# A decoder layer on one core: T4 is formed from T2 and B21, and the norms take their constant from a padded column

## The chip, the cores and the metric

The kernel runs on one core of one Trainium2 chip. Its time is the time on the device, in microseconds (us), from one launch to its end; the metric is the median over runs. Five engines work side by side, each through its own instructions in order: PE (TensorE, matmuls), DVE (VectorE, elementwise work), ACT (ScalarE, functions, copies and roundings), POOL (GpSimd) and SP (SyncE). SP, POOL and ACT also issue transfers (DMAs). An instruction that waits for another engine holds up everything behind it on its own engine.

## The reference

The depth is one, so of the four token mixers only the first (multi-scale causal pooling) runs, and then the gated ConvFFN. There are 1024 positions of 1024 features, a hidden width of 2816, and everything is float32.

```python
def rms_norm(x, g):
    xf = x.astype(jnp.float32)
    y = xf * lax.rsqrt(jnp.mean(xf * xf, axis=-1, keepdims=True) + EPS)
    return (y * g.astype(jnp.float32)).astype(x.dtype)

def pool_mixer(x, w, b, scale):
    ...
    for gi, w_len in enumerate(POOL_WINDOWS):          # 2, 4, 8, 16; 256 features each
        ...
        groups.append(window_sum / count - xf[..., gi * POOL_GROUP:(gi + 1) * POOL_GROUP])
    d = jnp.stack(groups, axis=2)
    y = jnp.einsum('bsgc,gcd->bsgd', d, w.astype(jnp.float32)).reshape(bsz, seq, D_MODEL) + b
    return (scale * y).astype(x.dtype)

def conv_ffn(x, w_in, conv_w, conv_b, w_out):
    h = causal_depthwise_conv(x @ w_in, conv_w, conv_b)
    val, gate = jnp.split(h, 2, axis=-1)
    return (jax.nn.silu(gate) * val) @ w_out

# the one layer
h = rms_norm(x, norm_mix_g)
x = x + pool_mixer(h, ...)
x = x + conv_ffn(rms_norm(x, norm_ffn_g), ...)
```

## The kernel before

**The first stage** takes the positions in eight tiles of 128, j = 0 to 7, in a software pipeline (the loop at L496): while tile j is normed and windowed, tile j-2 goes through the mixer's weights and tile j-4 becomes an operand of the feed-forward part. Per tile: ACT squares and sums x (`junk_a`, statistic `st_a`), DVE scales the window matrix by the norm (`bandr`), PE forms the window sums (`psd`), ACT copies them out (`dh`), PE multiplies by the pooling weights and adds the bias (`psy`), DVE adds x to give x1, which SP stores to DRAM (L268). x1 gets its own statistic (`junk_b`, `st_b`), DVE forms the normed tile (`n2`, printed as n_0 to n_7 in the program's order), and PE transposes it (`pst`). The last 16 rows of each tile reach the next one through a small extra product (`edge_band`, `ps_edges`, with a norm of its own, `st_e`).

**A norm's statistic** (`rstd_of`) is, with m the sum of squares: s = sqrt(m + D·EPS) on ACT (L158), m + D·EPS on DVE (L159), q = s·s + that on DVE (L161), 1/q on DVE (L162); s and 1/q are then used together as scales. There are eight of these for x (`a0` to `a7`), eight for x1 (`b0` to `b7`) and one for the edges (`e`).

**The second stage** multiplies by `w_in` with a seven-product scheme of the Strassen-Winograd kind. The normed, transposed activations are four quarters: B11 and B12 are the first 512 features for positions 0 to 511 and 512 to 1023, B21 and B22 the other 512 features. They lie in one tile, `n2f`. The operands are B11, B21, B22 and the sums T1 = B11 - B12, T3 = B22 - B12, T2 (minus the sum of B22 and T1, made in place of B22) and T4 = B22 - B21 + T1. In tiles j = 4 to 7, `ffn_operand` forms T1 from the first 512 features (L306), rounds it with ACT (L313) and leaves the remainder with DVE (L314): every operand is a rounded part and a remainder. It also forms T3 (L308) and B22 - B21 (L309), in 128-column pieces. T2 and T4 are made later, after the loop (L542 and L549), in two halves each.

The weights' side is 22 chunks n of 128 by 1024 (`win`), of which sums S1 to S4 are needed besides A11, A12 and A22. For the first two chunks these sums are made by accumulating DMAs that POOL issues (L336), later by DVE (L328). Each chunk's seven products (`step`, L374) go to the banks X, Y and Z; the first two chunks' products are interleaved so that P1 and P2 (B11, B21) come before the ones that need T1 (`Z<-T,S1s`), and T2, T3 and T4 last (L436 to L438). The chunk's outputs are then put together by DVE, convolved, gated and stored. **The third stage** does the same scheme with `w_out` (L731).

**What sets the order.** The code is written against a layer that records all operations and orders them itself, by a model of durations, holding to what the code asks with `issue_after`. A part that is left out or moved to another engine therefore changes the order of its neighbours too. Waits between engines come from that layer as well. The lines of the loop's end that the later steps turn on are:

```python
    for ks in halves:
        nc.vector.scalar_tensor_tensor(b22[:, ks], b22[:, ks], -1.0, t1[:, ks], op0=ALU.mult, op1=ALU.subtract)
        split_n(nops["T2"], b22[:, ks], ks=ks)
    event(7)
    event(8)
    for ks in halves:
        split_n(nops["T3"], t3[:, ks], ks=ks)
    for ks in halves:
        add(t4[:, ks], t4[:, ks], t1[:, ks])
        split_n(nops["T4"], t4[:, ks], ks=ks)
```

Of the kernel before, what the change touches and what calls it, by code (L numbers as in the profile page):

```python
# [7 lines left out]
F32 = mybir.dt.float32  # L8
F32R = mybir.dt.float32r
BF16 = mybir.dt.bfloat16  # L10
AF = mybir.ActivationFunctionType
ALU = mybir.AluOpType
PSUM = bass.MemoryType.PSUM

P = 128
S = 1024
D = 1024
# [8 lines left out]
EPS = 1e-6  # L26
# [15 lines left out]
XBUFS = 5  # L42
# [6 lines left out]
def trunk_kernel(ctx: ExitStack, tc: tile.TileContext, x, consts, par, rows, pool_w, w_in, w_out, out):  # L49
    nc = tc.nc  # L50
# [6 lines left out]
    hls = ctx.enter_context(tc.tile_pool(name="hls", bufs=1))  # L57
# [4 lines left out]
    pp = pre.enter_context(tc.tile_pool(name="pre", bufs=1))  # L62
# [17 lines left out]
        return t  # L80


    xs = {}

    def load_x(j):
        if j < 2 or j >= 2 + XBUFS:
            xs[j] = hls.tile([P, D], F32, tag="hl", name=f"x{j}", bufs=7)
        else:
            xs[j] = pp.tile([P, D], F32, tag="x", name=f"x{j}", bufs=XBUFS)
        nc.sync.dma_start(xs[j], x[j * P : (j + 1) * P, :])  # L90

    cst = pp.tile([P, BD], F32, tag="cst", name="cst")
# [7 lines left out]
    scale = rows_raw[:, 0, :GRP]  # L100
# [49 lines left out]
    ident = cst[:, ID:]  # L150

    marks = {}

    def rstd_of(src, name):
        junk = pp.tile([P, D], BF16, tag="junk", name=f"junk_{name}")
        st = pp.tile([P, 4], F32, tag="st", name=f"st_{name}", bufs=8)
        nc.scalar.activation(junk, src, AF.Square, accum_out=st[:, 0:1])
        marks[name] = nc.scalar.activation(st[:, 1:2], st[:, 0:1], AF.Sqrt, bias=eps_t).ins  # L158
        nc.vector.tensor_scalar(st[:, 0:1], st[:, 0:1], D * EPS, None, op0=ALU.add)  # L159

        nc.vector.scalar_tensor_tensor(st[:, 3:4], st[:, 1:2], st[:, 1:2], st[:, 0:1], op0=ALU.mult, op1=ALU.add)  # L161
        nc.vector.reciprocal(st[:, 2:3], st[:, 3:4])  # L162
        return st[:, 1:2], st[:, 2:3]
# [4 lines left out]
    bands, stats = {}, {}  # L168
# [84 lines left out]
    n2s = {}  # L253
# [16 lines left out]
            mixer_out_stats(j)  # L270

    def mixer_out_stats(j):
        n2s[j] = (n2s[j], rstd_of(n2s[j], f"b{j}"))

    def ffn_norm(j):
        x1, r = n2s[j]
# [13 lines left out]
    def ffn_operand(j):  # L290
        n2 = n2s.pop(j)
        ps = bank2(f"pst{j}")
        for c in range(NK):
            nc.tensor.transpose(ps[:, c * P : (c + 1) * P], n2[:, c * P : (c + 1) * P], ident)  # L294
        cols = slice(j * P, (j + 1) * P)
        ps3 = ps.rearrange("p (c s) -> p c s", c=NK)
        lo, hi = slice(0, 4), slice(4, 8)
        if j < NS // 2:
            split_n(nops["B11"], ps3[:, lo, :], cols)
            split_n(nops["B21"], ps3[:, hi, :], cols)  # L300
            nc.scalar.activation(n2f[:, :, cols], ps3, AF.Copy)
            return
        cols0 = slice(cols.start - NH, cols.stop - NH)
        b11, b12, b21, b22 = n2f[:, lo, cols0], ps3[:, lo, :], n2f[:, hi, cols0], n2f[:, hi, cols]
        nc.scalar.activation(b22, ps3[:, hi, :], AF.Copy)
        sub(b11, b11, b12)  # L306
        split_n(nops["T1"], b11, cols0)
        sub(n2f[:, lo, cols], b22, b12)  # L308
        sub(b21, b22, b21)  # L309

    def split_n(t, src, cols=slice(None), ks=slice(None)):
        h = t[:, 0, ks, cols]
# [11 lines left out]
    def sub(out, a, b):  # L324
        nc.vector.tensor_tensor(out, a, b, ALU.subtract)  # L325

    def add(out, a, b):
        nc.vector.tensor_tensor(out, a, b, ALU.add)  # L328
# [125 lines left out]

    def stat(j):
        if j in xs and j not in stats:
            stats[j] = rstd_of(xs[j], f"a{j}")

    scale_b = scale_rows()
    stat(0)  # L460
# [73 lines left out]
    t1, t3, b22, t4 = n2f[:, lo, s0], n2f[:, lo, s1], n2f[:, hi, s1], n2f[:, hi, s0]  # L534
# [11 lines left out]
    for ks in halves:  # L546
        split_n(nops["T3"], t3[:, ks], ks=ks)
    for ks in halves:
        add(t4[:, ks], t4[:, ks], t1[:, ks])  # L549
        split_n(nops["T4"], t4[:, ks], ks=ks)  # L550
    mid.close()
    late_stack = ExitStack()
# [123 lines left out]
    for k in range(-SLOOK, len(oevents)):  # L676
# [9 lines left out]
        with tc.issue_after(lasts[-1]) if lasts else nullcontext():  # L686
# [12 lines left out]
            p, f = oevents[k]  # L699
# [26 lines left out]
        for i, g, c, bank in steps:  # L726
            a, b = oops[p, g]
# [88 lines left out]
```

## Time and profile before

| | |
|---|---|
| runs | 700.93, 700.96 and 701.71 us; median 700.96 us |
| profiled execution | span 699.1 us, first to last instruction; what its launch adds outside the span is not shown. The median is 1.9 us above the span |
| TensorE clock granted | 1.000 of full |
| busy: PE | 692.5 us of 699.1 |
| busy: DVE | 597.9 us |
| busy: ACT | 343.0 us |
| busy: POOL | 13.3 us |

By stage, in busy us:

| stretch | what runs | PE | DVE | ACT |
|---|---|---|---|---|
| 0 to 65 | the eight tiles | 63.23 of 65 | 46.59 | 45.78 |
| 65 to 130 | the last operands, chunks 0 to 2 | 63.53 of 65 | 64.80 | 37.66 |
| 130 to 486 | the other chunks | 356.00 of 356 | 303.96 | 167.30 |
| 486 to 699 | the product with `w_out` | 209.72 of 213 | 182.51 | 92.25 |

A row of the timeline has the start and the length in us, the engine, the line of the kernel, the operation, output<-input, the shape and the count; what stands in brackets at its end is idle time of the engine just before, and what ended it. Several equal instructions are one row. A matmul is pipelined: the row's length reaches to the modelled end of the last of them, and the next one may start before that; the pitch from start to start is what a matmul costs.

### The profile page before, as it was taken

The numbers are of one execution on the slowest core, as the hardware profiler recorded it, in microseconds if no ns is written. First come the engines' busy times: TensorE is split into PE (matmuls) and PEld (weight loads), VectorE is DVE, ScalarE is ACT, GpSimd is POOL, SyncE is SP. The second block draws the span as 40 slices with busy tenths as digits, with TensorE's granted clock in tenths as the row PEclk, the third lists the DMA queues.
The fourth block names the chain that finished last, engine by engine and source line by source line (L and its number), as shares of the span: only waits on it lengthen the run. The fifth ranks groups of instructions, "written<-read, shape, count | busy, mean of one in ns | idle before, by whom it ended". The sixth has DMA issues, their size and how long they took to land.

```text
span 699.1 us, 8512 instructions
## 1 busy us (share of the span) xinstructions
PE 692.5 (99%) x3164; PEld 575.8 (82%) x3164; DVE 597.9 (86%) x883; ACT 343.0 (49%) x515; POOL 13.3 (2%) x33
## 2 busy tenths in 40 slices
PE   9999999999999999999999999999999999999998
PEld 7898778888888888888888888888888888888886
DVE  4798999999888888888888888876887988999985
ACT  6686645554454454444454444444454344444431
POOL 3020000000000000000000000000000000000000
PEclk9999999999999999999999999999999999999999
DMA  8964112322212112222222212229989700122231
GB/s 279 304 170 121 61 60 91 120 91 91 90 64 89 68 57 86 91 91 90 91 90 91 91 69 82 97 87 350 326 301 339 269 22 0 61 90 89 63 106 61
DMA packets 32562, 85.49 MB, mean 122 GB/s; under 512 B 3692, under 2 KB 5384, under 8 KB 29704
## 3 DMA queue, kind: packets, MB, share of 16 engines
q1 hardware_dynamic: 31328, 82.83, 33.3%
q0 software_dynamic: 1184, 2.11, 1.7%
q8 instruction: 25, 0.41, 0.2%
q14 instruction: 17, 0.14, 0.1%
q10 hardware_dynamic: 8, 0.00, 0.0%
HBM read 62.89 MB, written 19.92 MB: 118 GB/s over the span
## 4 chain that ended last, share of the span: by engine, by line
PE 98%; DVE 1%; ACT 0%; issue 0%; POOL 0%; DVEq 0%; POOLq 0%
PE oP L731 30%; PE Y L374 26%; PE Z L374 17%; PE X L374 16%; PE psy L261 4%; PE psd L179 2%; PE pst L294 1%; PE psy L264 1%; DVE n2f L325 0%; PE idle_ps L133 0%; PE ps_scale L199 0%; DVE T L314 0%; PE ps_edges L179 0%; PE ps_gain L225 0%; DVE n L279 0%; DVE S4s L77 0%
## 5 line engine op out<-in xcount | busy, mean ns | idle before, releaser
L731 PE MATMUL oP<-oBP,oAP 128*128 128x512 f32 (+1 forms) x924 | 208.9, 388 | 0.0
L731 PEld LDWEIGHTS oP<-oBP,oAP 128*128 128x128 f32 x924 | 172.9, 188 | 36.0 <-DVE oBP L77 0.3
L374 PE MATMUL Z<-T,S1s 128*128 128x512 f32 x264 | 64.0, 390 | 1.5 <-ACT T L313 1.2
L374 PE MATMUL X<-B,A11s 128*128 128x512 f32 x264 | 64.3, 390 | 0.0
L374 PE MATMUL Y<-T,S2s 128*128 128x512 f32 x264 | 64.0, 390 | 0.0
L374 PE MATMUL X<-B,A12s 128*128 128x512 f32 x264 | 63.5, 390 | 0.0
L374 PE MATMUL Y<-T,S3s 128*128 128x512 f32 x264 | 63.4, 389 | 0.0
L374 PE MATMUL Y<-T,A22s 128*128 128x512 f32 x264 | 63.4, 389 | 0.0
L374 PE MATMUL Z<-B,S4s 128*128 128x512 f32 x264 | 63.2, 389 | 0.0
L374 PEld LDWEIGHTS Z<-T,S1s 128*128 128x128 f32 x264 | 49.3, 188 | 12.6 <-ACT T L313 1.7
L374 PEld LDWEIGHTS Y<-T,S2s 128*128 128x128 f32 x264 | 49.4, 188 | 10.8 <-ACT S2s L76 0.4
L374 PEld LDWEIGHTS Y<-T,S3s 128*128 128x128 f32 x264 | 49.5, 188 | 10.3
L374 PEld LDWEIGHTS Z<-B,S4s 128*128 128x128 f32 x264 | 49.6, 188 | 10.3
L374 PEld LDWEIGHTS Y<-T,A22s 128*128 128x128 f32 x264 | 49.6, 188 | 10.3
L374 PEld LDWEIGHTS X<-B,A12s 128*128 128x128 f32 x264 | 49.5, 188 | 10.2
L374 PEld LDWEIGHTS X<-B,A11s 128*128 128x128 f32 x264 | 49.4, 188 | 10.2
L76 ACT ACTIVATE oBP<-blk 128x512 fp32r<-128x512 f32 x53 | 33.5, 633 | 49.1 <-PE oP L731 32.2
L77 DVE TENSOR_TENSOR oBP<-blk,oBP 128x512 fp32r<-128x512 f32 x53 | 36.6, 691 | 13.0 <-ACT oBP L76 13.0
L432 ACT ACTIVATE gate<-gate 128x1024 f32<-128x1024 f32 x22 | 23.4, 1061 | 44.8 <-DVE gate L423 44.5
L76 ACT ACTIVATE oAP<-blk 128x512 fp32r<-128x512 f32 x55 | 34.1, 621 | 18.9 <-DVE blk L325 15.9
L328 DVE TENSOR_TENSOR win<-win 128x512 f32<-128x512 f32 x60 | 41.2, 687 | 1.1
L77 DVE TENSOR_TENSOR oAP<-blk,oAP 128x512 fp32r<-128x512 f32 x55 | 37.7, 685 | 2.6 <-ACT oAP L76 2.6
(129 smaller groups left out, 940.7 us busy)
## 6 DMA issues: line engine op xcount, KB each, us to landing
win<-in_w_in_dram SPq DMA_DIRECT2D x22, 1024.0 KB, 4.8
g_dram<-val SPq DMA_DIRECT2D x22, 512.0 KB, 2.6
blk<-g_dram SPq DMA_DIRECT2D x33, 256.0 KB, 5.3
blk<-in_w_out_dram SPq DMA_DIRECT2D x31, 256.0 KB, 5.9
A12s<-g_dram SPq DMA_DIRECT2D x22, 256.0 KB, 4.9
B21s<-in_w_out_dram SPq DMA_DIRECT2D x22, 256.0 KB, 2.6
x<-in_x_dram SPq DMA_DIRECT2D x8, 512.0 KB, 5.5
x_dram<-x SPq DMA_DIRECT2D x8, 512.0 KB, 2.8
```

The source lines that it names most:

```text
L76: nc.scalar.activation(t[:, 0, :], src, AF.Copy)
L77: m = nc.vector.tensor_tensor(t[:, 1, :], src, t[:, 0, :].bitcast(F32), ALU.subtract)
L179: m = nc.tensor.matmul(ps[:, c * P : (c + 1) * P], src[:, c * P : (c + 1) * P], weights[:, c // 2, :], start=True, stop=True)
L261: nc.tensor.matmul(o, dh[:, c, :], wps[:, c, :], start=c % 4 == 0, stop=False, skip_group_check=True)
L264: m = nc.tensor.matmul(ps[:, cols], ones, bias_hl[:, cols], start=False, stop=True, skip_group_check=True)
L294: nc.tensor.transpose(ps[:, c * P : (c + 1) * P], n2[:, c * P : (c + 1) * P], ident)
L328: nc.vector.tensor_tensor(out, a, b, ALU.add)
L374: nc.tensor.matmul(bank, a[:, i, ks], b[:, l, k, :], start=opens and m == 0, stop=m == 11, skip_group_check=not opens)
L432: nc.scalar.activation(gate, gate, AF.Silu)
L731: nc.tensor.matmul(bank, a[:, u, i * P : (i + 1) * P], b[:, v, c], start=opens and first, stop=g == NP2 - 1 and m == 2, skip_group_check=n ...
```

## The change

Three things are changed.

1. **The x tiles have one column more.** `load_x` makes them 128 by 1025; DVE sets the last column to sqrt(D·EPS) (`memset`, eight of 128x1). Everything else uses the first 1024 columns, as before.
2. **A norm's statistic** for x and x1 is `rstd_padded`. ACT squares and sums all 1025 columns, so the sum m holds the constant already: s = sqrt(m) has no bias operand, and DVE's addition (L159) is gone. q = s·s + m is one ACT instruction for x tiles 2 to 7 and all eight x1 tiles (`Identity` with the scale s and the bias m, both per-partition operands); for x tiles 0 and 1 it stays a DVE instruction. The reciprocal stays on DVE. The edges' norm keeps the old form.
3. **T4 is formed from T2 and B21.** L309's four differences B22 - B21 (128x4x128 each) are left out, and the two halves of T4 are (-1)·T2 - B21, where T2 is the tile that has taken B22's place. The instruction is a `scalar_tensor_tensor` where it was an addition of the same size.

```diff
-    xs = {}
+    xs, padded = {}, {}
 
     def load_x(j):
         if j < 2 or j >= 2 + XBUFS:
-            xs[j] = hls.tile([P, D], F32, tag="hl", name=f"x{j}", bufs=7)
+            padded[j] = hls.tile([P, D + 1], F32, tag="hl", name=f"x{j}", bufs=7)
         else:
-            xs[j] = pp.tile([P, D], F32, tag="x", name=f"x{j}", bufs=XBUFS)
+            padded[j] = pp.tile([P, D + 1], F32, tag="x", name=f"x{j}", bufs=XBUFS)
+        nc.vector.memset(padded[j][:, D:], (D * EPS) ** 0.5)
+        xs[j] = padded[j][:, :D]
         nc.sync.dma_start(xs[j], x[j * P : (j + 1) * P, :])
...
+    def rstd_padded(src, name, on_act):
+        junk = pp.tile([P, D + 1], BF16, tag="junk", name=f"junk_{name}")
+        st = pp.tile([P, 4], F32, tag="st", name=f"st_{name}", bufs=8)
+        ms, root, q, inv = (st[:, i : i + 1] for i in range(4))
+        nc.scalar.activation(junk, src, AF.Square, accum_out=ms)
+        marks[name] = nc.scalar.activation(root, ms, AF.Sqrt).ins
+        if on_act:
+            marks[name] = nc.scalar.activation(q, root, AF.Identity, bias=ms, scale=root).ins
+        else:
+            nc.vector.scalar_tensor_tensor(q, root, root, ms, op0=ALU.mult, op1=ALU.add)
+        nc.vector.reciprocal(inv, q)
+        return root, inv
...
     def mixer_out_stats(j):
-        n2s[j] = (n2s[j], rstd_of(n2s[j], f"b{j}"))
+        n2s[j] = (n2s[j], rstd_padded(padded.pop(j), f"b{j}", True))
...
         sub(n2f[:, lo, cols], b22, b12)
-        sub(b21, b22, b21)
...
     def stat(j):
         if j in xs and j not in stats:
-            stats[j] = rstd_of(xs[j], f"a{j}")
+            stats[j] = rstd_padded(padded[j], f"a{j}", j > 1)
...
     for ks in halves:
-        add(t4[:, ks], t4[:, ks], t1[:, ks])
+        nc.vector.scalar_tensor_tensor(t4[:, ks], b22[:, ks], -1.0, t4[:, ks], op0=ALU.mult, op1=ALU.subtract)
         split_n(nops["T4"], t4[:, ks], ks=ks)
```

The lines of the changed kernel are numbered on: L267 is L282 there, L279 is L294, L313 and L314 are L327 and L328, L325 is L339, L328 is L342, L374 is L388.

**How the order moves, first place: DVE around the last tiles' T1.** x_229 is x1 of the last tile, n_7 its normed tile, pst_749 (pst_738 after) its transposes; T_155 (T_158) is T1, and the rows `T<-n2f,T` are remainders of T1's pieces. Before:

```order
L325 TENSOR_TENSOR n2f<-n2f 128x4x128
L279 SCALAR_TENSOR_TENSOR n_7_701<-x_229,st_b_695,gain_b 128x1024
L314 TENSOR_TENSOR T_155<-n2f,T_155 128x4x128
L77 TENSOR_TENSOR S1s_796<-win_546,S1s_796 128x512
L77 TENSOR_TENSOR S4s_799<-win_421,S4s_799 128x512
L77 TENSOR_TENSOR S4s_802<-win_546,S4s_802 128x512
L325 TENSOR_TENSOR n2f<-n2f,pst_749 128x4x128 x2
L325 TENSOR_TENSOR n2f<-n2f 128x4x128
L77 TENSOR_TENSOR S2s_805<-win_421,S2s_805 128x512
L314 TENSOR_TENSOR T_155<-n2f,T_155 128x4x128
L77 TENSOR_TENSOR S3s_822<-S_0_423,S3s_822 128x512
```

The same stretch of DVE's order with the change:

```order
L328 TENSOR_TENSOR T_158<-n2f,T_158 128x4x128
L294 SCALAR_TENSOR_TENSOR n_7_692<-x_234,st_b_687,gain_b 128x1024
L77 TENSOR_TENSOR S1s_784<-win_541,S1s_784 128x512
L77 TENSOR_TENSOR S4s_787<-win_420,S4s_787 128x512
L77 TENSOR_TENSOR S4s_790<-win_541,S4s_790 128x512
L77 TENSOR_TENSOR S2s_793<-win_420,S2s_793 128x512
L339 TENSOR_TENSOR n2f<-n2f,pst_738 128x4x128 x2
L77 TENSOR_TENSOR S3s_810<-S_0_422,S3s_810 128x512
L328 TENSOR_TENSOR T_158<-n2f,T_158 128x4x128
```

The two differences are gone, T1's remainder of tile 6 stands ahead of n_7 where it stood behind it, and T1's last remainder now has S3s ahead of it where it stood ahead of S3s.

**Second place: ACT at the same point.** pst_749 (pst_738) is the last tile's transpose, B_791 (B_779) is the operand B22, in two halves, T_155 (T_158) is T1. Before:

```order
L76 ACTIVATE S2s_805<-win_421 128x512
L76 ACTIVATE S3s_822<-S_0_423 128x512
L305 ACTIVATE n2f<-pst_749 128x4x128
L313 ACTIVATE B_791<-n2f 128x1024 x2
L313 ACTIVATE T_155<-n2f 128x4x128
L76 ACTIVATE A22s_844<-win_421 128x512
```

With the change:

```order
L76 ACTIVATE S2s_793<-win_420 128x512
L414 ACTIVATE ha_764<-X_658 128x512
L76 ACTIVATE S3s_810<-S_0_422 128x512
L320 ACTIVATE n2f<-pst_738 128x4x128
L327 ACTIVATE B_779<-n2f 128x1024
L327 ACTIVATE T_158<-n2f 128x4x128
L327 ACTIVATE B_779<-n2f 128x1024
```

T1's last rounded piece has one half of B22 ahead of it, where it had both.

**Third place: DVE where chunk 2's sums are made.** win_847 (win_835) is the chunk's weights; the second `win<-win` row is the sum S2, which the product `Y<-T,S2s` of chunk 2 needs; val_972 (val_960) is chunk 0's convolution. Before:

```order
L77 TENSOR_TENSOR A11s_935<-win_847,A11s_935 128x512
L314 TENSOR_TENSOR T_792<-n2f,T_792 128x1024
L328 TENSOR_TENSOR S_2_952<-win_847 128x512
L411 TENSOR_TENSOR hb_950<-r_838,Y_905 128x512
L328 TENSOR_TENSOR win_847<-win_847 128x512
L422 SCALAR_TENSOR_TENSOR val_972<-ha_776,par_sb,val_972 128x1023
L328 TENSOR_TENSOR win_847<-win_847 128x512
L423 SCALAR_TENSOR_TENSOR val_972<-ha_776,par_sb,val_972 128x1022
L77 TENSOR_TENSOR S2s_956<-win_847,S2s_956 128x512
```

With the change:

```order
L328 TENSOR_TENSOR T_780<-n2f,T_780 128x1024 x2
L77 TENSOR_TENSOR A11s_923<-win_835,A11s_923 128x512
L425 TENSOR_TENSOR hb_938<-r_826,Y_893 128x512
L342 TENSOR_TENSOR S_2_940<-win_835 128x512
L436 SCALAR_TENSOR_TENSOR val_960<-ha_764,par_sb,val_960 128x1023
L342 TENSOR_TENSOR win_835<-win_835 128x512
L437 SCALAR_TENSOR_TENSOR val_960<-ha_764,par_sb,val_960 128x1022
L342 TENSOR_TENSOR win_835<-win_835 128x512
```

Both of val's steps stand ahead of the sum S2 now, where one did; T4's second remainder stands ahead of A11s, where it stood behind.

## The prediction

> **What bounds the kernel now.** I read the page first, then the table of waits, then the timeline around each wait, one engine at a time.
>
> ```profile
> span 699.1 us, 8512 instructions
> PE 692.5 (99%) x3164; PEld 575.8 (82%) x3164; DVE 597.9 (86%) x883; ACT 343.0 (49%) x515; POOL 13.3 (2%) x33
> ```
>
> PE is idle for 6.6 us of its 699.1. The change touches no matmul, so all it can win is idle time of PE, and all it can cost is new idle time. The waits of PE say where that idle time is:
>
> ```profile
> PE Z L374 <- ACT T L313: 1.2, 1, 1.2
> PE Z L374 <- DVE T L314: 0.2, 1, 0.2
> ```
>
> The rest is PE's start, a short wait at the edges' product, which depends on PE itself, and the last outputs; the change does not shorten these. So one place matters, the first product with T1. PE's rows there in the timeline, and from the chain of waits one row for the pitch of these matmuls:
>
> ```profile
> 68.84 3.56 PE L374 MATMUL X<-B,A12s 128*128 128x512 f32 x15
> 72.37 1.07 PE L294 MATMUL pst<-cst,n 128*128 128x128 f32 x8
> 73.19 2.30 PE L374 MATMUL X<-B,A12s 128*128 128x512 f32 x9
> 76.73 0.73 PE L374 MATMUL Z<-T,S1s 128*128 128x512 f32 x2 [1.24 <-ACT T L313]
> 77.69 5.28 PE L374 MATMUL Z<-T,S1s 128*128 128x512 f32 x22 [0.23 <-DVE T L314]
> ```
>
> ```profile
> 129.62 2.72 PE Z L374 x12
> ```
>
> The pitch is 2.72 / 12 = 0.227 us. The idle times in brackets count from a modelled end and are too small. By pitch, nine matmuls from 73.19 are through at 75.23, and the next starts at 76.73: 1.50 lost. Two more are through at 77.18, the next starts at 77.69: 0.51. Fifteen from 68.84 are through at 72.24, pst follows at 72.37: 0.13. Together **2.1 us**, the most that can be won here.
>
> **What is late there.** DVE's and ACT's rows ahead of it:
>
> ```profile
> 67.49 0.68 DVE L325 TENSOR_TENSOR n2f<-n2f 128x512 f32<-128x512 f32 x1
> 67.62 0.63 ACT L313 ACTIVATE T<-n2f 128x512 fp32r<-128x512 f32 x1
> 68.09 0.14 DVE L159 TENSOR_SCALAR st_b<-st_b 128x1 f32<-128x1 f32 x1
> 68.29 0.69 DVE L314 TENSOR_TENSOR T<-n2f,T 128x512 fp32r<-128x512 f32 x1
> 68.90 0.21 DVE L161 SCALAR_TENSOR_TENSOR st_b<-st_b 128x1 f32<-128x1 f32 x1
> 70.35 0.68 DVE L325 TENSOR_TENSOR n2f<-n2f 128x512 f32<-128x512 f32 x1
> 70.95 1.27 DVE L279 SCALAR_TENSOR_TENSOR n<-x,st_b,gain_b 128x1024 f32<-128x1024 f32 x1
> 74.15 2.00 ACT L313 ACTIVATE B<-n2f 128x1024 fp32r<-128x1024 f32 x2
> 74.56 1.27 DVE L325 TENSOR_TENSOR n2f<-n2f,pst 128x512 f32<-128x512 f32 x2
> ```
>
> The last tile's n must be made (70.95), transposed (72.37), subtracted into T1 (74.56), rounded by ACT (until 76.67, behind two B22 roundings) and its remainder formed by DVE (until 77.64). DVE works without a gap through it; its 128x512 rows follow each other every 0.60.
>
> **The change, part by part.** *Differences B22 - B21.* Four go, each 0.60 of DVE (67.49 to 68.09 is one). Two lie in the rows above, ahead of n; the fourth lies behind n and ahead of T1's remainder.
>
> *The statistic.* For the last tile L159 (68.09 to 68.29, 0.20) and L161 (0.1 to 0.2) leave DVE's queue too. So 0.60 + 0.20 + 0.15 + 0.60 = 1.55 goes ahead of n. The order puts T1's remainder of tile 6, 0.60, ahead of n. Net 0.95. The remainder at 68.29 begins as ACT's piece ends (67.62 + 0.63), and ACT gives that piece hardly sooner, so I take off 0.15 for waiting and put **n at 70.15**, 0.8 earlier.
>
> *PE's side.* PE has pst after 12 of those matmuls instead of 15, at 68.84 + 2.72 = 71.56; n ends at 70.15 + 1.27 = 71.4, so the 0.13 goes. PE then wants T1 at about 75.2.
>
> *T1's last piece.* After n come S1s, two S4s and S2s: 70.15 + 1.20 + 4 × 0.60 = 73.75 for the subtraction (74.56 before), the first half done at 74.4. On ACT one half of B22 is ahead now, not two; about 73.7 to 74.7. So T1's rounded piece runs 74.65 to 75.25, and PE starts at 75.3: 0.1 lost instead of 1.50. The remainder has S3s ahead of it: 73.75 + 3 × 0.60 = 75.55, done at 76.25. PE's first two matmuls are through at 75.75, and it waits to 76.3: 0.55 instead of 0.51. Of 2.1 us about 0.65 to 0.8 stays: **a gain of 1.3 at this place**.
>
> *What is late next.* DVE has no free time behind this place (64.80 busy of 65 in the table by stage), so PE, being 1.3 earlier, runs into what DVE feeds it. The first product that hangs on a sum of DVE is chunk 2's S2:
>
> ```profile
> 100.51 0.68 DVE L328 TENSOR_TENSOR win<-win 128x512 f32<-128x512 f32 x1
> 101.11 1.27 DVE L423 SCALAR_TENSOR_TENSOR val<-ha,par_sb,val 128x1022 f32<-128x1022 f32 x1
> 102.31 0.68 DVE L77 TENSOR_TENSOR S2s<-win,S2s 128x512 fp32r<-128x512 f32 x1
> 101.29 0.63 ACT L76 ACTIVATE S2s<-win 128x512 fp32r<-128x512 f32 x1 [2.41 <-DVE win L328]
> 101.98 0.73 PE L374 MATMUL Y<-T,S2s 128*128 128x512 f32 x2
> ```
>
> The sum at 100.51 is followed at once by ACT's rounding and by PE: 1.47 from one start to the other. From n (70.95) to the sum DVE works 29.56. With the change the fourth difference is out of it (-0.60), T1's remainder of tile 6 too (-0.60, it now precedes n), and val's second step is put ahead of the sum (101.11 to 102.31, +1.20): 70.15 + 29.56 = 99.71, PE at 101.18. That is **0.8 earlier** than 101.98, and PE, 1.3 earlier, waits for it. The smaller of the two gains counts: 0.8. From there on I see nothing that holds PE: it has no wait in the table after T1.
>
> *T4's instruction* takes the same:
>
> ```profile
> L542 DVE SCALAR_TENSOR_TENSOR n2f<-n2f 128x1024 f32<-128x1024 f32 x2 | 2.4, 1216 | 0.0
> L328 DVE TENSOR_TENSOR n2f<-n2f 128x1024 f32<-128x1024 f32 x2 | 2.4, 1215 | 0.0
> ```
>
> L542 is the form that T4 gets, L328 the one it had. It needs T2 finished, which already precedes it on DVE.
>
> *What is added.* Eight memsets of one column, and q on ACT:
>
> ```profile
> 1.15 0.06 DVE L107 MEMSET eps_t<- 128x1 f32 x1
> 3.12 0.20 ACT L110 ACTIVATE warm<-eps_t 128x1 f32<-128x1 f32 x1
> L158 ACT ACTIVATE st_b<-st_b,eps_t 128x1 f32<-128x1 f32 x8 | 2.3, 286 | 0.0
> L421 ACT ACTIVATE val<-ha,par_sb 128x1024 f32<-128x1024 f32 x22 | 27.4, 1246 | 7.0 <-DVE T L314 1.8 <-DVE ha L405 1.7 <-issue 1.0
> ```
>
> The memsets are 0.06 each, three while DVE waits for x and five between weights that PE takes later: nothing; without that cover 0.5. The root without a bias costs 0.20 (L110) and not 0.29. For q the trace has no row. It is L421's form, two per-partition operands, on one column: 1.25 less 1024 columns at about 0.4 per 512 (two 128x1024 roundings 2.00, one 128x512 0.63), so 0.4 to 0.45. Bounds are 0.20 (no operand) and 0.45; I take 0.4. ACT thus gets 0.3 more per norm, 14 times, 4.2 us. Most of it falls into ACT's idle time (45.78 busy of 65). One place has little cover, the edges:
>
> ```profile
> 17.65 0.55 DVE L166 TENSOR_SCALAR edge_band<-cst,st_e 128x512 f32<-128x512 bf16 x1
> 18.43 1.95 PE L179 MATMUL ps_edges<-edge_band,x_edge 128*128 128x128 f32 x16
> ```
>
> The edges' statistic follows tile 2's on ACT, so edge_band ends at 18.20 + 0.3 = 18.50, and PE wants it at 18.43: **0.1 lost**, which all later rows share. With q at 0.20 nothing is lost.
>
> **The sum.** -0.8 + 0.1 = -0.7 on the span of 699.1: 698.4. The median of the runs stands 1.9 above the span, and nothing changes that: 700.96 - 0.7 = 700.26, said as **700.2 us**. Two medians of this kernel are told apart from about 0.2%, 1.4 us, so this forecast is "the same".
>
> **The rivals.**
>
> *The gain at T1 is kept, or the whole wait goes.* If DVE has more in hand at S2 than I count, 1.3 - 0.1 = 1.2 is won: 699.8. For it: DVE's 29.56 is counted, not seen to be all needed. Against: ACT waited 2.41 for that very sum. If T1's remainder too comes in time, 2.1 - 0.1 = 2.0: 699.0. Against: S3s stands ahead of that remainder and alone costs 0.60.
>
> *ACT becomes the bound among the tiles.*
>
> ```profile
> 35.00:45.00 10.00, 10.00 (x66) 9.11 (x65) 9.54 (x25) 9.55 (x18) 2.78 (x4) 1.00 0.62 165
> ```
>
> ACT (fourth pair) is busy 9.55 of 10 there, and a tile takes 6.6 us; two norms per tile add 0.6, the idle time per tile is 0.3. ACT falls back 0.3 per tile, about 0.5 in this stretch. Against: PE ran this stretch without idle time, so its inputs lie ahead. If nothing lay ahead, 0.5 of the 0.7 is given back: 700.7. The Trainium skill, page "ScalarE: Activation LUTs", section "Rules for kernel authors", speaks against this part of the change: additions and multiplications belong on VectorE, not on ScalarE. By that rule q was better left on DVE; the row above gives it a case in this stretch alone.
>
> *The accumulating DMAs come too late (slower).* SP now issues S_0's load behind x1's store of tile 1, not ahead of it.
>
> ```profile
> 20.21 0.94 SPq L341 DMA_DIRECT2D S<-in_w_in_dram  x1
> 27.27 0.33 SPq L268 DMA_DIRECT2D x_dram<-x  x1
> 28.48 0.89 POOL L336 DMA_DIRECT2D S<-win  x1 [21.32 <-DMA S<-in_w_in_dram]
> 37.10 0.87 POOL L336 DMA_DIRECT2D win<-win  x1 [7.72 <-DMA S<-win]
> 43.98 1.74 POOL L336 DMA_DIRECT2D win<-win  x2 [5.12 <-PE psy L264]
> 55.88 1.16 ACT L76 ACTIVATE S1s<-win 128x512 fp32r<-128x512 f32 x2
> DMA to landing us min/median/max: 3.3/3.7/8.1
> ```
>
> DVE now makes x1 of tile 1 ahead of n_0, so the store goes out up to 1 us sooner than 27.27, and the load at about 26.5: POOL's chain shifts by 6.3: 34.8, 43.4, and the last sum that S1s needs at 50.3 with 3.7 to land: 54.0, where chunk 1's S1s wants it at 56.4. Hidden, with 2.4 to spare. If the later transfers take 8.1 each, that sum lands at about 60.6, ACT stands still for 4.2, and the norm of tile 6 queues behind it; there some 3 us are spare, so PE loses 1.3 or more: 701.5, up to 703. It decides from 5 us of extra lateness on.
>
> **How the numbers follow.** Forecast (699.8 to 700.7) 0.55; the gain at T1 kept, about 699.6 to 699.8, 0.18; the whole wait gone, 0.08; ACT gives most of it back, 700.7 to 701.1, 0.11; late sums or another new wait, above 701.1, 0.08. Faster than 699.56 (0.2%): 0.08 and a quarter of 0.18, so 0.13. Slower than 702.36: half of the last and some unknown, 0.07. The rest, 0.80, is the same. The range leaves out the best half of the second rival and the worst of the last: 699.1 to 701.5.
>
> **What would show it.** Right: PE's first `Z<-T,S1s` follows X within 0.2, its remainder costs about 0.5, `Y<-T,S2s` of chunk 2 starts about 0.7 earlier and waits longer for ACT's S2s; q at 0.4; ps_edges 0.1 late. Wrong: Z waits over 1 us, PE idle anywhere between 20 and 64, a wait of POOL's sums at S1s, or Y at the old time.

## The result and the profile after

The changed kernel takes **716.13 us** (median of 4 runs, 715.97 to 716.61); the kernel before, measured with it, 701.23 (4 runs, 700.93 to 701.71). The ratio is 1.0214, with a 95% interval of 1.0202 to 1.0227: slower, by 15 us. The forecast of 700.2 and its range to 701.5 were wrong by far more than any rival allowed. The profiled execution took 716.27 us.

The head of its page and its table of waits (columns: who waited for whom; us in total, times, longest):

```profile
span 714.4 us, 8506 instructions
PE 708.6 (99%) x3164; PEld 575.7 (81%) x3164; DVE 594.1 (83%) x857; ACT 345.4 (48%) x529; POOL 13.5 (2%) x33
```

```profile
PE ps_edges L194 <- ACT st_a L161: 0.5, 1, 0.5
...
PE Z L388 <- DVE T L328: 0.3, 1, 0.3
```

The span is 15.3 us longer. PE's idle time is not: 714.4 - 708.6 = 5.8 us, against 6.6 before, and the wait of 1.2 for ACT's T1 is gone. PE is **busy** for 16.1 us more, with the same 3164 matmuls. So the matmuls themselves became slower. The groups by line show which (busy us, mean ns of one); first before, then after:

```profile
L731 PE MATMUL oP<-oBP,oAP 128*128 128x512 f32 (+1 forms) x924 | 208.9, 388 | 0.0
L374 PE MATMUL X<-B,A11s 128*128 128x512 f32 x264 | 64.3, 390 | 0.0
L374 PE MATMUL X<-B,A12s 128*128 128x512 f32 x264 | 63.5, 390 | 0.0
```

```profile
L745 PE MATMUL oP<-oBP,oAP 128*128 128x512 f32 (+1 forms) x924 | 214.5, 394 | 0.0
L388 PE MATMUL X<-B,A11s 128*128 128x512 f32 x264 | 65.8, 397 | 0.0
L388 PE MATMUL X<-B,A12s 128*128 128x512 f32 x264 | 64.3, 392 | 0.0
```

Stage three and six of the seven products of stage two are 5 to 7 ns longer for one matmul; the seventh, `A12s`, only 2. The numbers that they multiply are as they were but for rounding. There are 2763 such matmuls (float32r, 512 columns; with nine of 256 columns that are in the first group too it is the 2772 of the expectations below), and 16.1 us over 2763 is 5.8 ns for one. The pitch can be read in PE's timeline, where each row starts when the one before is through its last start:

```profile
115.88 2.94 PE L388 MATMUL Y<-T,S3s 128*128 128x512 f32 x12
118.65 2.96 PE L388 MATMUL Z<-B,S4s 128*128 128x512 f32 x12
121.45 0.63 PE L388 MATMUL X<-B,A11s 128*128 128x512 f32 x2
```

Twelve take 2.77 and 2.80 here, not 2.72: 0.231 to 0.233 us for one. The granted clock is 0.999, as good as before, and the plain float32 products of the first stage keep their pace (`psy<-wps` 380 ns, `psd` 275 and `pst` 273 for one, before and after). What is left that all slow matmuls share is where their operands lie.

**The layout.** In the kernel before, the operand tiles of both stages lie in SBUF at multiples of 4096 bytes from each other: three of 16384 bytes, then the seven shared buffers (tag `hl`) of 4096, then four of 16384. x0, x1 and x7 share the tag `hl`. With the padded column an x tile has 4100 bytes, the tag's size is rounded up to 4128, so the seven buffers are 4128 bytes apart and what lies behind them moves by 7 x 32 = 224 bytes. No trace shows addresses; these are those of the two kernels as built. They also fit the odd one out: in the changed kernel 240 of the 264 matmuls of `A12s` still have their two operands at a multiple of 256 bytes from each other; of all the other float32r products only 12 matmuls have.

### The profile page after: what moved, and what is told of

Same layout as the page of the kernel before. It is cut to its first block, busy times and chain, and to the rows that moved or that the text cites. A ratio compares the mean times of both kernels' runs of the same rounds, so it can differ in the third digit from the quotient of the medians.

```text
span 714.4 us, 8506 instructions
## 1 busy us (share of the span) xinstructions
PE 708.6 (99%) x3164; PEld 575.7 (81%) x3164; DVE 594.1 (83%) x857; ACT 345.4 (48%) x529; POOL 13.5 (2%) x33
## 4 chain that ended last, share of the span: by engine, by line
PE 95%; DMA 2%; DVE 1%; ACT 1%; issue 0%; DVEq 0%
PE oP L745 30%; PE Y L388 26%; PE Z L388 17%; PE X L388 16%; PE psy L276 3%; DMA x<-in_x_dram 2%; PE psd L194 1%; PE pst L309 1%; DVE n2f L339 1%; PE psy L279 0%; ACT junk_a L160 0%; PE ps_edges L194 0%; DVE T L328 0%; DVE S1s L77 0%; DVE S4s L77 0%
## 5 line engine op out<-in xcount | busy, mean ns | idle before, releaser
L745 PE MATMUL oP<-oBP,oAP 128*128 128x512 f32 (+1 forms) x924 | 214.5, 394 | 0.0
L388 PE MATMUL Z<-T,S1s 128*128 128x512 f32 x264 | 65.7, 395 | 0.3 <-DVE T L328 0.3
L388 PE MATMUL X<-B,A11s 128*128 128x512 f32 x264 | 65.8, 397 | 0.0
L388 PE MATMUL Y<-T,S2s 128*128 128x512 f32 x264 | 65.5, 396 | 0.0
L388 PE MATMUL Y<-T,A22s 128*128 128x512 f32 x264 | 65.1, 395 | 0.0
L388 PE MATMUL Z<-B,S4s 128*128 128x512 f32 x264 | 65.0, 395 | 0.0
L388 PE MATMUL Y<-T,S3s 128*128 128x512 f32 x264 | 64.7, 394 | 0.0
L388 PE MATMUL X<-B,A12s 128*128 128x512 f32 x264 | 64.3, 392 | 0.0
L388 PEld LDWEIGHTS Z<-T,S1s 128*128 128x128 f32 x264 | 49.3, 187 | 13.0 <-DVE T L328 0.7
L388 PEld LDWEIGHTS Y<-T,S2s 128*128 128x128 f32 x264 | 49.5, 188 | 12.3 <-ACT S2s L76 0.4
L388 PEld LDWEIGHTS Y<-T,A22s 128*128 128x128 f32 x264 | 49.5, 188 | 12.0
L388 PEld LDWEIGHTS X<-B,A11s 128*128 128x128 f32 x264 | 49.5, 188 | 12.0
L388 PEld LDWEIGHTS Z<-B,S4s 128*128 128x128 f32 x264 | 49.6, 188 | 11.8
L388 PEld LDWEIGHTS Y<-T,S3s 128*128 128x128 f32 x264 | 49.7, 188 | 11.4
L388 PEld LDWEIGHTS X<-B,A12s 128*128 128x128 f32 x264 | 49.5, 188 | 11.3
L76 ACT ACTIVATE oAP<-blk 128x512 fp32r<-128x512 f32 x55 | 34.1, 620 | 19.8 <-DVE blk L339 16.1
L342 DVE TENSOR_TENSOR win<-win 128x512 f32<-128x512 f32 x60 | 41.2, 688 | 1.1
```

What stands on the lines that cost most here:

```text
L76: nc.scalar.activation(t[:, 0, :], src, AF.Copy)
L388: nc.tensor.matmul(bank, a[:, i, ks], b[:, l, k, :], start=opens and m == 0, stop=m == 11, skip_group_check=not opens)
L745: nc.tensor.matmul(bank, a[:, u, i * P : (i + 1) * P], b[:, v, c], start=opens and first, stop=g == NP2 - 1 and m == 2, skip_group_check=n ...
```

## The experiments

### The layout alone, with no other change

```diff
-            xs[j] = hls.tile([P, D], F32, tag="hl", name=f"x{j}", bufs=7)
+            xs[j] = hls.tile([P, D + 1], F32, tag="hl", name=f"x{j}", bufs=7)[:, :D]
```

> The kernel before, with one thing changed: x0, x1 and x7 are allocated one column wider and only their first 1024 columns are used, so that the seven shared buffers lie 4128 bytes apart instead of 4096 and everything behind them 224 bytes further on. No instruction is added, removed or moved. Theory A (the place of the two operands in SBUF sets the pitch of the f32r matmuls): 0.233 us instead of 0.227, 2772 x 6 ns = 16 us more, about 716.5 us, with the idle time of PE as before. Theory B (the new work on DVE and ScalarE slows PE's matmuls): 701.2 us and 0.227. Theory C (only the shift of the four later operand tiles by 224 bytes matters): slower too, but in stage two alone, 4 of 7 products, some 6 us.

Measured: 716.49 us, ratio 1.0217 (1.0203 to 1.0231). The order on every engine is that of the kernel before, row for row. Two of its groups:

```profile
L731 PE MATMUL oP<-oBP,oAP 128*128 128x512 f32 (+1 forms) x924 | 214.0, 394 | 0.0
L374 PE MATMUL Z<-T,S1s 128*128 128x512 f32 x264 | 65.5, 395 | 1.4 <-ACT T L313 1.2 <-DVE T L314 0.2
```

The old wait for T1 is there (1.2 and 0.2) and the matmuls are as slow as in the changed kernel. The whole loss comes from 4100 bytes in the place of 4096. Theory B falls. This kernel has the layout of the changed one and none of its other parts: 716.49 (715.78 to 716.97) against 716.13 (715.97 to 716.61), so on the same layout the rest of the change is worth 0.4 us or nothing; the runs overlap.

### Only what lies behind the buffers is moved

```diff
     hls = ctx.enter_context(tc.tile_pool(name="hls", bufs=1))
+    gap = ctx.enter_context(tc.tile_pool(name="gap", bufs=1)).tile([P, 56], F32, tag="gap", name="gap")
```

> The kernel before, with an unused tile of 224 bytes behind the seven shared buffers: these stay 4096 apart, and only what lies behind them (the operands T2, T3, B22, T4 among it) moves by 224 bytes. Theory A: stage three, where both operands are shared buffers, stays at 0.227; in stage two the 4 of 7 products whose moving operand has shifted may rise towards 0.233, at most 1056 x 6 ns = 6.3 us, so 701 to 708 us. Theory B: 701.2. Theory C: the same loss in stage two as the kernel with wider x tiles, and nothing more in that one.

Measured: 708.87 us, ratio 1.0106 (1.0091 to 1.0122). Its groups:

```profile
L731 PE MATMUL oP<-oBP,oAP 128*128 128x512 f32 (+1 forms) x924 | 208.8, 388 | 0.0
L374 PE MATMUL Y<-T,S2s 128*128 128x512 f32 x264 | 65.6, 396 | 0.0
L374 PE MATMUL Y<-T,S3s 128*128 128x512 f32 x264 | 65.2, 396 | 0.0
L374 PE MATMUL Y<-T,A22s 128*128 128x512 f32 x264 | 65.1, 395 | 0.0
L374 PE MATMUL Z<-B,S4s 128*128 128x512 f32 x264 | 65.0, 396 | 0.0
L374 PE MATMUL X<-B,A11s 128*128 128x512 f32 x264 | 64.8, 392 | 0.0
```

Stage three (L731), where both operands are shared buffers at 4096 from each other, is at its old 388. The products with the moved T2, T3, T4 and B22 (S2s, S3s, A22s, S4s) are at 395 to 396, and the product with B11, which has not moved, is nearly at its old pace: 392. So it is the place of the two operands against **each other** that counts. The loss of 7.6 us is 1.3 above the most that I had put on it: the moved products pay up to 7 ns and not 6, and the unmoved ones up to 2, for which no run shows the reason. Theory C has the moved tiles right, but they are only half of it: the buffers' own spacing is left for the other half of the 15 us, and 5.2 of that is seen in stage three (208.8 here, 214.0 with the layout alone).

### The pitch by the operands' places, alone

A kernel that computes nothing of the reference, and copies x to its output: one tile of ones, sets of 36 matmuls in the order of stage three, and the stationary operand moved against the moving one. This probe and the two that follow are one execution each.

```python
("d0b", 0, 8192), ..., ("d32b", 32, 8192), ...      # name, byte of the stationary, byte of the moving operand
for f in range(3):
    for i in range(4):
        for m, (u, v) in enumerate(((0, 0), (0, 1), (1, 0))):
            matmul(ps[:, i*512:(i+1)*512], big[:, a0 + u*512 + i*128 : ... + 128], big[:, b0 + v*512 : ... + 512])
```

> Not the kernel's computation: the output is a copy of x. Sets of 36 f32r matmuls 128x512 in the order of stage three, four PSUM banks by three products, all on one large SBUF tile of ones. Between sets only the place of the stationary operand against the moving one changes (d0b to d16384b: shifted by so many bytes; both32b: both shifted together), and the last four sets run while DVE and ScalarE copy at full load. Theory A: 36 x 0.227 = 8.17 us for d0b and for multiples of some power of two up to 4096, 8.3 to 8.5 for d32b, d64b, d96b and the like; both32b like d0b. Theory B: 8.17 for every quiet set, and more only in the four with copies beside them. If all sets are alike at 8.17, the place alone does not do it.

PE's rows of its timeline; a row's length has the pipeline's tail of 0.16 in it, the differences between rows are free of it:

```profile
32.88 8.33 PE L70 MATMUL d0b<-big 128*128 128x512 f32 x36
...
57.81 8.55 PE L70 MATMUL d32b<-big 128*128 128x512 f32 x36
66.20 8.56 PE L70 MATMUL d64b<-big 128*128 128x512 f32 x36
...
116.42 8.33 PE L70 MATMUL d256b<-big 128*128 128x512 f32 x36
124.59 8.55 PE L70 MATMUL d288b<-big 128*128 128x512 f32 x36
...
215.84 8.32 PE L70 MATMUL d16384b<-big 128*128 128x512 f32 x36
...
232.17 8.71 PE L70 MATMUL both4b<-big 128*128 128x512 f32 x36
...
249.01 8.37 PE L70 MATMUL both32b<-big 128*128 128x512 f32 x36
...
314.80 8.33 PE L70 MATMUL busy0b<-big 128*128 128x512 f32 x36
322.96 8.55 PE L70 MATMUL busy32b<-big 128*128 128x512 f32 x36
```

A shift of 32 or 64 bytes costs 0.22 over 36 matmuls, 6 ns each, as in the kernel. 256, 512 and 16384 cost nothing, 288 costs what 32 does. Sets without a shift that were repeated through the run agree within 0.01. Both operands shifted together by 32 (8.37), 64, 128 or 256 lose about 1 ns or less. Shifted together by 4 they lose nearly 11 (8.71), and by 16 or 48 about 3, though their distance is as before; so the distance is not all that counts. In the kernels here every operand starts at a multiple of 32, and the distance is what the padded column changed. With DVE and ACT copying at full load beside it (the busy rows) nothing changes: the cause lies within PE's own two operands. So theory A holds without anything else of the kernel.

The Trainium skill, page "SBUF — State Buffer", section "Operand start alignment", gives the rule for start addresses (a multiple of the element size) and says "This is about legality, not speed"; these runs put the speed beside it, 6 ns of 227. The same page, section "SBUF: two separate sides", has it that PE never waits for other engines at SBUF, with which the busy rows agree, and the table under "A bandwidth-pool intuition that's wrong (but worth ruling out)" gives the weight loads a read port of their own, independent of the moving operand's. Taken to mean that the two reads share nothing, a shift of one operand against the other would cost nothing; here it costs 6 ns, and the measurement decides.

### What kinds of matmul it concerns

The same construction, no part of the reference computed. own0next32 (its row reads own0next, the last digits are dropped): every matmul's own operands lie 0 apart and the next stationary block 32 off; own32next0 (own32next): the reverse. The bf sets have bf16 operands, the full sets twelve plain float32 matmuls, each of which the trace has as two.

> Not the kernel's computation: the output is a copy of x. Sets of 36 matmuls on one SBUF tile as in the first sets of this kind. own0next32: each matmul's own two operands lie at a multiple of 256 bytes from each other, but the stationary operand that is loaded while it runs lies 32 bytes off; own32next0: the reverse. If the two reads that collide are the moving stream and the next weights, own0next32 takes 8.40 us and own32next0 8.16; if a matmul's own operands matter, the reverse; if both are long, any mixture costs. The e sets fill in other shifts: 8.16 only at a multiple of 256, 8.2 to 8.3 at 208 or 176 if there is a slope towards 192. For bf16 operands, 256 columns and plain fp32 I have no forecast from a row; if the two read streams collide only when a matmul needs operands at full rate, plain fp32 (four passes) shows nothing.

PE's rows of its timeline:

```profile
107.87 8.33 PE L68 MATMUL e240b<-big 128*128 128x512 f32 x36
...
124.34 8.56 PE L68 MATMUL own0next<-big 128*128 128x512 f32 x36
132.73 8.56 PE L68 MATMUL own32next<-big 128*128 128x512 f32 x36
...
149.32 7.94 PE L68 MATMUL bf0b<-big 128*128 128x512 bf16 x36
...
172.64 7.93 PE L68 MATMUL bf32b<-big 128*128 128x512 bf16 x36
...
232.90 10.46 PE L68 MATMUL full0b<-big 128*128 128x512 f32 x24
243.20 10.46 PE L68 MATMUL full32b<-big 128*128 128x512 f32 x24
```

bf16 and plain float32 don't care; float32r with 512 columns does. Both mixtures are slow, so "the next block's load collides" is not shown, nor its reverse. And 240 is free here (in the next probe it costs 1.7 ns), which no rule by 256 foresees.

### A map in steps of four bytes

The same construction again, with 24 matmuls to a set, the shift in the name (m sets), one stationary block for all matmuls (fix), and 384 columns (c384).

> Not the kernel's computation: the output is a copy of x. Sets of 24 f32r matmuls on one SBUF tile of ones: the stationary operand shifted against the moving one by every multiple of 4 bytes from 0 to 256 (m sets), back by 32 to 240 (neg), with one and the same stationary block throughout (fix), with 256, 384 and 448 columns (c), and with the shift only against the matmul's own operand or only against the next one's (own, next). If a simple stagger of 256 bytes decides, 24 x 0.227 = 5.44 us at 0, 240 and 256 alone and 5.5 to 5.6 elsewhere, neg32 like a shift by 224 and neg240 like 16; if the two reads collide only while a new stationary block is loaded, fix32 is like fix0. If some shift is faster than 5.40 us, the kernel's present layout is not the best one, and 2772 matmuls would gain the difference.

PE's rows of its timeline:

```profile
37.47 5.61 PE L132 MATMUL m0b<-big 128*128 128x512 f32 x24
42.92 5.74 PE L132 MATMUL m4b<-big 128*128 128x512 f32 x24
...
204.82 5.61 PE L132 MATMUL m120b<-big 128*128 128x512 f32 x24
...
265.78 5.87 PE L132 MATMUL m164b<-big 128*128 128x512 f32 x24
...
393.77 5.62 PE L132 MATMUL m256b<-big 128*128 128x512 f32 x24
...
443.44 5.75 PE L132 MATMUL fix32b<-big 128*128 128x512 f32 x24
...
468.63 4.33 PE L132 MATMUL c384d0b<-big 128*128 128x384 f32 x24
472.80 4.33 PE L132 MATMUL c384d32b<-big 128*128 128x384 f32 x24
```

No placement is faster than 0: the kernel's layout is already the best of these. Most shifts cost 2 to 11 ns per matmul (164 the most), without an order that I can name; 120, 144, 156, 204, 228 and 252 are free by the same reading. fix32 uses one and the same stationary block throughout and is slow too, so it isn't the change to a new block that collides. The trace has a weight load ahead of each of its 24 matmuls all the same, so a collision with the load itself is not ruled out. Mixtures as above with 64 and 128 bytes cost 1 to 4 ns. With 384 columns the difference is under 1 ns, with 448 at most 2. What the two streams share, and why a few odd shifts are free, stays open; that distances of multiples of 256 are free, for a moving operand that stays where it is, is shown by every one that was tried (0, 256, 512, 1024, 2048, 4096, 16384).

### The change without its layout

First with the seven buffers at 4096: x0, x1 and x7 unpadded, their norms (6 of 16) as before, all else as in the change.

```diff
-            padded[j] = hls.tile([P, D + 1], F32, tag="hl", name=f"x{j}", bufs=7)
+            xs[j] = hls.tile([P, D], F32, tag="hl", name=f"x{j}", bufs=7)
...
```

> The changed kernel with the shared buffers back at 4096 bytes: x0, x1 and x7 are 1024 columns wide, and their norms (6 of the 16) are made as before; the other ten norms have the padded column and s*s+m on ScalarE, and T4 is made from T2 and B21. Theory A: pitch 0.227, and the time that I had forecast for the change, 700.2 us, or up to 1 us less. Theory B: about 711 to 716 us, since most of the new work is still there. Theory C: 700.2 as well.

Measured: 701.05 us, ratio 0.9997 (0.9988 to 1.0006). The pitch is back, the gain of 0.7 is not there. Its waits for T1:

```profile
PE Z L388 <- ACT T L327: 1.2, 1, 1.2
PE Z L388 <- DVE T L328: 0.2, 1, 0.2
```

They are those of the kernel before. I took tile 7's norm for the reason, which stands ahead of T1 and has its old form in this kernel; that is argued and not shown. ACT's order is that of the kernel before too: both halves of B22 (from 74.81) go ahead of T1's last piece (76.72), and the section on T1 shows what that does. So x7 went to the padded tiles, and the room was taken from `bandr`, which moved into buffers that lie idle there; on top of the edit above:

```diff
-XBUFS = 5
+XBUFS = 6
...
-        t = bands[j] = pp.tile([P, NG, P], F32, tag="bandr", name=f"bandr{j}", bufs=2)
+        t = bands[j] = work.tile([P, NG, P], F32, tag="q1", name=f"bandr{j}", bufs=2)
```

> The change without its layout: the seven shared buffers are 4096 bytes apart again, x7 goes to the padded x tiles (six buffers instead of five), the room for it comes from bandr, which moves into two buffers of the same size that lie idle among the tiles, and only the norms of tiles 0 and 1 keep the old form. T4 is made from T2 and B21. Theory A (the layout is the whole loss, the rest works as I had forecast): pitch 0.227, PE's first product with T1 starts about 0.7 us sooner than before against its own pipeline, and the time is 701.2 less 0.4 to 1.6: 699.6 to 700.8. Rival (the new work costs PE something of its own behind the layout): 701.2 or more at a pitch of 0.227.

Measured: 701.00 us, ratio 0.9997 (0.9988 to 1.0006). The waits for T1 are 0.6 (ACT) and 0.7 (DVE), and the edges' product waits 0.7. Against its own first X (58.68, before 57.59) Z starts 0.7 earlier (77.10, before 76.73), as theory A had it, but of that only 0.35 is left at chunk 2's S2s (102.72, before 101.98). Again no gain in the time, and less than theory A gave it. This is not the changed kernel with another layout alone: its order on ACT has both halves of B22 ahead of T1's last piece again. The next one takes tile 2's s*s+m back to DVE:

```diff
-            stats[j] = rstd_padded(padded[j], f"a{j}", j > 1) if j in padded else rstd_of(xs[j], f"a{j}")
+            stats[j] = rstd_padded(padded[j], f"a{j}", j > 2) if j in padded else rstd_of(xs[j], f"a{j}")
```

> As the kernel with the aligned layout, but s*s+m of tile 2's first norm is made by DVE. It tests one step: in the changed kernel the edges' product started 0.45 us later than before, and behind ScalarE's 0.39 us for tile 2 stood the edges' statistic. If that is the reason, ps_edges starts 0.3 sooner than in the kernel with the aligned layout and the time is 0.3 less; if x2's arrival sets it, nothing changes.

Measured: 700.54 us, ratio 0.9990 (0.9981 to 0.9999). ps_edges starts at 18.71 in place of 19.28. Of these 0.57 us 0.15 is x2's statistic, which began at 13.72 and not 13.87; the rest is ACT's 0.39 ahead of the edges' statistic. Not all of the wait belongs to the change: the kernel with the layout alone, whose statistics are the old ones, has a wait there too, for the square of x2:

```profile
PE ps_edges L179 <- ACT junk_a L157: 0.3, 1, 0.3
```

That is x2's arrival. From the start of x2's statistic to ps_edges it takes 5.08 us there, 5.41 in the changed kernel and 4.99 with tile 2 on DVE: 0.33 is the change's own cost. The statistic itself began anywhere from 12.99 to 13.97 in the traces of this document, at 13.22 in the kernel before and at 13.97 with the layout alone, where the instructions are the same.

### T4 alone, and the order at T1

First T4's part of the change on the kernel before:

```diff
-        sub(b21, b22, b21)
...
-        add(t4[:, ks], t4[:, ks], t1[:, ks])
+        nc.vector.scalar_tensor_tensor(t4[:, ks], b22[:, ks], -1.0, t4[:, ks], op0=ALU.mult, op1=ALU.subtract)
```

> The kernel before with one part of the change: the four differences B22 - B21 are left out and T4 is made as -T2 - B21. Norms and buffers as before, so the pitch stays at 0.227 in every theory that goes by the layout. Two differences of 0.60 us leave DVE ahead of the last tile's n: PE's wait for T1 shrinks by 0.5 to 1.0 us, 700.3 to 700.8. If the numbers that T4 holds or the other order on DVE made PE's matmuls slower, more than 701.2.

Measured: 701.03 us, ratio 0.9997 (0.9988 to 1.0006). The wait at T1 did not shrink at all. ACT's and PE's rows there:

```profile
74.49 2.01 ACT L312 ACTIVATE B<-n2f 128x1024 fp32r<-128x1024 f32 x2
...
76.41 0.61 ACT L312 ACTIVATE T<-n2f 128x512 fp32r<-128x512 f32 x1
...
77.07 0.73 PE L373 MATMUL Z<-T,S1s 128*128 128x512 f32 x2 [1.21 <-ACT T L312]
```

Both halves of B22 are rounded ahead of T1's last piece, though B22 is wanted 6 us later. In the changed kernel the order put one half behind (its rows):

```profile
74.24 1.06 ACT L327 ACTIVATE B<-n2f 128x1024 fp32r<-128x1024 f32 x1
...
75.21 0.61 ACT L327 ACTIVATE T<-n2f 128x512 fp32r<-128x512 f32 x1
...
75.97 0.63 PE L388 MATMUL Z<-T,S1s 128*128 128x512 f32 x2
```

So at T1 ACT's order seems to decide when Z starts, more than DVE's work does. The next kernels issue B22's pieces behind T1's last one on both engines:

```diff
     for ks in halves:
-        split_n(nops["B22"], b22[:, ks], ks=ks)
+        with tc.issue_after(marks["T1"][0]), tc.issue_after(marks["T1"][1]):
+            split_n(nops["B22"], b22[:, ks], ks=ks)
...
```

> The kernel before with one order changed: the roundings and remainders of B22 are issued behind T1's last piece on ScalarE and on DVE. No work is added or left out. Theory A (as in the prediction: what is won at T1 runs into DVE's sum for chunk 2's S2): the wait for T1 falls from 1.7 us to some 0.6, and PE gives most of it back at that sum, since DVE's work up to it is the same; 700.6 to 701.1. Rival (ScalarE's order was the whole reason of the wait and nothing limits behind it): 700.0.

Measured, on the kernel before: 701.04 us, ratio 0.9997 (0.9989 to 1.0006). PE's rows, and DVE's row of chunk 2's sum S2:

```profile
76.11 0.69 PE L374 MATMUL Z<-T,S1s 128*128 128x512 f32 x2 [0.46 <-ACT T L313]
77.22 5.28 PE L374 MATMUL Z<-T,S1s 128*128 128x512 f32 x22 [0.42 <-DVE T L314]
...
100.50 0.68 DVE L328 TENSOR_TENSOR win<-win 128x512 f32<-128x512 f32 x1
101.96 0.73 PE L374 MATMUL Y<-T,S2s 128*128 128x512 f32 x2
```

Z starts at 76.11 and not 76.73, the remainder 0.47 earlier too, and chunk 2's S2 stands at 101.96, where it stood before (101.98). DVE's sum comes at 100.50 (100.51 before), so the whole gain is given back: by pitch PE loses 0.2 among chunk 2's A11s products and 0.3 ahead of S2s. DVE's sums are the limit behind T1, as the prediction had it.

The same order on the kernel with T4's part:

> The kernel before without the four differences B22 - B21 and with T4 as -T2 - B21, and with B22's roundings behind T1's last piece. With the differences left out but the old order the wait at T1 had not shrunk (701.03 against 701.09). Theory A: it shrinks now to some 0.5, and since DVE has 2.4 us less to do ahead of chunk 2's S2, PE keeps it: 699.8 to 700.2. Rival (the order does not matter, DVE alone sets T1): 701.0.

Measured: 700.58 us, ratio 0.9992 (0.9983 to 1.0001). PE's wait for T1 is 0.5: Z starts no earlier after the first X than with the order alone (18.39 us in both), but the wait for the remainder is gone, which is DVE's part. Now PE also waits 0.2 at S2s of chunk 2 (102.13). That is about 0.6 us won where 0.9 to 1.3 was forecast, and it is not told apart from no change.

And on the change with the mended layout and tile 2's s*s+m on DVE:

> The change with the seven buffers at 4096 bytes, tile 2's s*s+m on DVE, and B22's roundings behind T1's last piece. Theory A: the waits of 0.6 and 0.7 us for T1 that the same kernel has without that order fall to 0.3 together: 700.54 - 1.0 = 699.5, from 699.2 to 699.9. Rival: PE meets DVE's sums later, 700.3 or more.

Measured: 700.50 us, ratio 0.9988 (0.9979 to 0.9997). The waits for T1 fall to 0.4, and PE waits 0.2 at chunk 2's S2s (101.61): the rival of that expectation, not theory A. It is the fastest of all, by 0.1% on the kernel before; its interval and that of the kernel with tile 2 moved are the two that lie below 1, both only just.

Last, all of s*s+m on DVE:

```diff
-            stats[j] = rstd_padded(padded[j], f"a{j}", j > 2) if j in padded else rstd_of(xs[j], f"a{j}")
+            stats[j] = rstd_padded(padded[j], f"a{j}", False) if j in padded else rstd_of(xs[j], f"a{j}")
...
-        n2s[j] = (n2s[j], rstd_padded(padded.pop(j), f"b{j}", True) if j in padded else rstd_of(n2s[j], f"b{j}"))
+        n2s[j] = (n2s[j], rstd_padded(padded.pop(j), f"b{j}", False) if j in padded else rstd_of(n2s[j], f"b{j}"))
```

> As the one before, but s*s+m is made by DVE in all norms (0.22 us of DVE in place of 0.39 of ScalarE, 12 norms). If ScalarE is what counts at T1 and at the edges, it is 0.1 to 0.3 us faster than with ScalarE; if DVE does, as much slower; both lie within what five rounds tell apart only if they add up.

Measured: 700.64 us, ratio 0.9993 (0.9985 to 1.0002). The edges' product starts at 18.25 without a wait, but x2's statistic began early in this execution (12.99), so that does not speak for DVE; and no difference in time can be told from s*s+m on ScalarE.

## Why the prediction was wrong

**The step that failed** stands in its first part: "The change touches no matmul, so all it can win is idle time of PE, and all it can cost is new idle time." The change touches the operands' places, and 2763 matmuls went from 0.227 to about 0.233 us: 16.1 us of busy PE, over 20 times the sum that was worked out. The words of the change said it (a padded column of each x tile), and the code showed that three x tiles share a tag with the matmuls' operands; I counted the memsets of that column and not its four bytes. No rival had a mechanism that makes PE busier.

**The rest of the sum held.** PE's idle time fell by 0.8, where the sum said 0.7; the slower PE, which comes later to each wait, has a part in that.

- *n and T1.* PE has pst after 12 matmuls and not 15 (72.28), Z starts at 75.97, 0.1 after X is through (73.08 + 12 x 0.233 = 75.88), and the remainder costs 0.43 (two matmuls from 75.97 are through at 76.44, the next starts at 76.87). Forecast: within 0.2, and 0.5. Against its own first X, Z starts 1.3 earlier; the gain forecast at this place was 1.3.
- *S2 of chunk 2.* `Y<-T,S2s` starts at 101.77. The whole timeline is 0.55 late since the edges (X at 58.14 and not 57.59), so against its own start it is 0.76 earlier; forecast 0.8. The run with only the order changed shows the same limit on the kernel before.
- *q on ACT* takes 0.38 (L163; forecast 0.4), the root without a bias 0.20 (L161), T4's form 1217 ns (L563; forecast 1216), a memset 0.06.
- *The edges* start at 18.88, 0.45 late; forecast 0.1. The 0.3 net of q and the shorter root is there, but x2's statistic began 0.25 later as well, and the 0.2 of cover that I counted on was used up by that. When x2 arrives is no work of the change, so this part of the miss is chance.
- *The rivals.* ACT is busy 9.97 of 10 from 35 to 45, as feared, but PE is not idle there. POOL's sums don't hold S1s up.

With the layout mended the change makes no difference that these runs can tell (701.0), but there the order at T1 is another, and only 0.35 is kept at S2. In the changed kernel itself 0.8 is kept at S2 and 0.55 lost ahead of it, some 0.25 of that by x2's late arrival; 0.25 to 0.5 us would be left. That is argued from the rows, and too small to be shown by the times.

## What to carry to other kernels

Before costing an edit by its instructions, look at what it does to the size of every tile that shares a tag or a pool with a matmul's operands: four bytes on an x tile moved ten operand tiles. For float32r matmuls with 512 columns keep the two operands at multiples of 256 bytes from each other and do not shift both by 4, 16 or 48 bytes, and when PE's busy time grows at the same number of matmuls, compare the mean ns of its groups before looking for waits. A gain of a microsecond at one wait is worth little until the next thing that ends last is known.

## What was not expected of the hardware

The pitch of a float32r matmul of 128x512 depends on the distance between its two operands in SBUF: about 227 ns at multiples of 256 bytes, 229 to 238 at most others, as fast as at 0 for a few odd ones (120, 204, 252), with or without the same stationary block, and also with DVE and ACT copying beside it. It depends on the place of the pair as well: both shifted together by 4 bytes cost nearly 11 ns, by 32 one. bf16 (0.216 us) and plain float32 show no dependence on the distance, float32r with 384 columns less than 1 ns. The mechanism isn't settled.
